# The second mixer of a two-layer diffusion backbone: its last group of modulation products behind the projections, and the output weights split on VectorE

## The chip, the core and the metric

The kernel runs on one core of one Trainium2 chip. The metric is the device time of one execution in microseconds. The program's engines are PE (TensorE, with its weight loads PEld), VectorE (DVE in the rows), ScalarE (ACT), GpSimd (POOL) and SyncE (SP), which issues nearly all DMAs from one queue in order.

## The reference

Two layers over 512 latent and 256 context tokens of width 1024. Each layer mixes (attention), adds the gated result, and passes the tokens through a mixture of 32 experts (2 per token). The second layer's mixer and its modulation are what matters here:

```python
mod = jax.nn.silu(c) @ w_mod[l] + b_mod[l]            # 1024 -> 6 * 1024, for c and for c_ctx
sh1, sc1, gt1, sh2, sc2, gt2 = jnp.split(mod[:, None, :], 6, axis=-1)
h_lat = modulate(x, norm_mix[l], sh1, sc1)
...
q, k, v = jnp.split(h @ w_in, 3, axis=-1)             # 8 heads, q and k in two halves of 64, v of 128
...
s = jnp.einsum('bqhcd,bkhcd->bhcqk', qi, k) * scale
p = jax.nn.softmax(s, axis=-1)
a = p[:, :, 0] - lam * p[:, :, 1]                     # differential attention
return jnp.einsum('bhqk,bkhe->bqhe', a, v)
...
x = x + gt1 * (rms_norm(o, subln) * (1 - lam_init)) @ w_out
tokens = modulate(x, norm_ffn[l], sh2, sc2)
x = x + gt2 * hier_moe(tokens, ...)
```

## The kernel before, in words

The stages follow one another: first mixer, its output projection with the router, experts, second mixer (`mixer_c`), its output projection, experts.

In `mixer_c` the normalised and modulated tokens are transposed and split into a high and a low part (`chh`, `chl`). For each of 8 heads, `in_proj` multiplies them by the head's weights (`wh`, `wl`; lines L264 to L266 by the helper `mm3`, three matmuls for one product at full precision) into one PSUM bank `pp`, which ScalarE empties (L689, L690). GpSimd applies the rope, VectorE the norm, and PE transposes the keys (`ptk`, L727) and, in `pack_q`, the queries (`ptq`, L582, from `qdup`). The attention runs in 32 units (8 heads by 4 tiles of 128 tokens). A unit has two score blocks on PE (L599 to L607), each followed by the maximum on VectorE (`nbias`, L1935), a scaling (L1945) and the exponential on ScalarE (L1939); then VectorE forms the factor `cf` (L1948, L1949) and the difference `p` (L1952), PE transposes it (`ptp`, L621), VectorE or ScalarE copies it (`pts`, L625), and PE multiplies it with the values (`po`, L636). VectorE normalises (L1964). Units of one head run beside the projections of later heads, so the projections end some way before the last units. When a tile of tokens has all heads, VectorE computes its norm (L287 to L299) and scales it (L1978).

Into this the mixer takes two jobs for the stage behind it. `mod_later` computes the columns of the modulation that `mixer_c` itself does not need, in groups of 2048 columns: group (1,1) holds `gt1` and `sh2`, group (1,2) `sc2` and `gt2`. A group has 8 blocks of weights of 1 MB, loaded by `mod_load` (L379) into the buffers `wr` (four, shared with the projection weights), multiplied on PE by `mod_mm` (L384, tile `pmod`), summed in pairs in a PSUM bank and added by VectorE into a row (L478). Group (1,2) is then scaled by the norm's gain (L494). SP stores the row (L500, `modrow`); the output projection reads it back (L1262 and L506). `prepare_out` loads the output weights (L1050, four blocks of 1 MB) and splits them in `split_ops`: ScalarE writes the high part (L325), another engine subtracts it from the weight (L328, tile `wo`).

The order of PE, VectorE, ScalarE and GpSimd is made at build time by the class `Sched`: each piece has an engine, an assumed duration, what it depends on, tokens that it takes and gives (`wr` for a weight buffer, `pt` and `pp` for PSUM banks, `mw` for modulation blocks in flight), and a position. An engine that is free takes the ready piece with the lowest position; unit j has position j. The modulation pieces are spread evenly from CM0 to CM1, and CMW is the number of `mw` tokens. On the chip each engine runs its list in order and waits by semaphores. The order of SP's queue is made by the framework.

Of the kernel before, what the change touches and what calls it, by code (L numbers as in the profile page):

```python
# [20 lines left out]
KD = 8  # L21
# [61 lines left out]
CPREP = 3.79  # L83
CPACK = 0.8
CP0 = -37.415
CMW = 1
CM0 = 1.0
CM1 = 28.601
DPE = .217
DDVE = 0.15  # L90
DACT = .119
# [147 lines left out]
class Backbone:  # L239
# [197 lines left out]
        return self.mod_columns(0, lambda: st["row"], [a], psp, tag)  # L437


    def mod_later(self, jobs, rows_tile, nf, silp, psp, tag, first, end, after):  # L440
        nc, S = self.nc, self.S
        total, n, out = KD * len(jobs), 0, {}
        ready = S.op("POOL", 0.5, lambda: self.mod_sil(silp), [after], pos=first)
        mms = [ready] * LA
        for l, g in jobs:
            st = {}
# [19 lines left out]
                st[k] = self.mod_load(l, g, k)  # L466

            def mm(k, st=st):
                if k % 2 == 0:
                    st["ps"] = psp.tile([128, 512], F32, tag=tag, name="pmod")  # L470
                self.mod_mm(st["ps"], silp, st[k], k, k % 2 == 0, k % 2 == 1)

            def add(k, l=l, g=g, st=st):
                r = st["row"]
                if k == 1 and (l, g) == (1, 0):
                    nc.vector.tensor_copy(r, st["ps"])
                else:
                    nc.vector.tensor_tensor(r, st["ps"], r, op=OP.add)  # L478

            S.pos = first + (end - first) * n / total  # L480
            a = S.op("POOL", 0.4, rows, [ready], take=("mrow",))
            a = S.op("DMA", 0.3, biases, [a])
            for k in range(KD):
                S.pos = first + (end - first) * n / total
                n += 1
                ld = S.op("DMA", 2.95, lambda k=k, load=load: load(k), [mms[-LA]], take=("wr", "mw"))
                mms.append(S.op("PE", 1.0, lambda k=k, mm=mm: mm(k), [ld, mms[-1]], take=() if k % 2 else ("pt",), give=("wr", "mw")))
                if k % 2:
                    a = S.op("DVE", 0.62, lambda k=k, add=add: add(k), [mms[-1], a], give=("pt",))
            if (l, g) == (1, 0):  # L490
                out[l, g] = self.mod_columns(l, lambda st=st: st["row"], [a], psp, tag, ("mrow",))
                continue
            if g == 2:
                a = S.op("DVE", 0.62, lambda st=st: nc.vector.scalar_tensor_tensor(  # L494
                    st["row"][0:64], st["row"][0:64], 1.0, nf[0:64], op0=OP.add, op1=OP.mult), [a])
# [518 lines left out]
    def prepare_out(self, l, wout, pos, after):  # L1014

        nc, S, i = self.nc, self.S, self.i
# [28 lines left out]
        for q in range(4):  # L1045
            S.pos = pos + 2 * q

            def load(q=q):
                w = parts[q] = self.wtile().rearrange("p (k f) -> p k f", k=2)
                nc.sync.dma_start(w, wout[q * 256:(q + 1) * 256].rearrange("(k p) f -> p k f", p=128))  # L1050

            ld = S.op("DMA", 2.95, load, [start], take=("wr",))
            for k in range(2):
                self.split_ops(lambda q=q, k=k: (*self.wo[2 * q + k], parts[q][:, k]), 1024, [ld], give=("wr",) if k else (),
                               low_on="POOL" if l else "DVE")


    def out_proj(self, l, oo, first, gain=None):
# [764 lines left out]
    def mixer_c(self, oo):  # L1823
        nc, tc, i = self.nc, self.tc, self.i
        S = self.S = Sched((DPE, DDVE, DACT, DPOOL), (EPE, EDVE, EACT, EPOOL), wr=NW, pt=2, s=2, po=1, pp=1, p0=2, p1=2, pts=2, qdup=1, qhl=2, rt=1, rt1=1, hss=2, khl=1,
                           grp=2, vv=3, whl=5, mrow=2, mw=CMW)
        keep, st = ExitStack(), ExitStack()
# [73 lines left out]
        for g in range(7):  # L1901
# [5 lines left out]

        room = [oo[:, 4 + m // 2, 512 * (m % 2):512 * (m % 2) + 512] for m in range(4)]
        rows = iter(room[0:2])
        self.mod_later([(1, 1), (1, 2)], lambda: next(rows), room[2], room[3][:, 0:256].rearrange("p (k f) -> p k f", k=KD),  # L1910
                       psm, "pt", CM0, CM1, S.op("-", 0.0, lambda: None, spare))
        prev = dict.fromkeys(("s", "t", "v"))
        packed, squares = {}, {t: [] for t in range(4)}
        for j, (g, t) in enumerate(units):
# [162 lines left out]
```

## Time and profile before

| | |
|---|---|
| median of 3 runs | 2040.12 us (2039.37 to 2042.49) |
| the profiled execution | 2038.13 us, its span 2036.3 us |
| PE, VectorE, ScalarE, GpSimd busy | 1767.3, 1023.2, 560.2, 355.5 us |
| granted TensorE clock, mean | 0.953 |
| second mixer, its output projection | from about 1031 us, from 1444.2 us |

The profile is one execution. Busy times are sums over the span; a stage's limit is read from its own stretch. Durations of matmuls overlap one another, so what a matmul costs is read from the starts of its neighbours. A wait is put down to what ended last.

### The profile page before, as it was taken

Reading aid. Unit: us, or ns where it says so; the run is one execution under the profiler, and the core shown is the slowest. Engines: PE = TensorE matmul, PEld = TensorE weight load, DVE = VectorE, ACT = ScalarE, POOL = GpSimd, SP = SyncE. Lnnn points to the kernel's source line nnn. Section 1 sums busy time; section 2 is a strip of 40 time slices with the busy share of each in tenths; the row PEclk is TensorE's granted clock in tenths of the full one; section 3 lists DMA queues with packets and bytes.
Section 4 is the critical chain, followed back from the end, with each engine's and each line's share of the span. In section 5 each row is a group of like instructions: output and inputs, shape, how many; then the busy total and the mean of one; then the engine's idle time right before and its main releaser. Section 6 shows DMA issues by size and latency. Waiting matters only on the chain. (4 is left out here: it accounts for less than half of the span.)

```text
span 2036.3 us, 27809 instructions
## 1 busy us (share of the span) xinstructions
PE 1767.3 (87%) x10130; PEld 1013.7 (50%) x10130; DVE 1023.2 (50%) x2621; ACT 560.2 (28%) x1280; POOL 355.5 (17%) x373
## 2 busy tenths in 40 slices
PE   4999998895999898998939999996878998988986
PEld 2798776684233222222228898885752332222222
DVE  4698878596333332323357877777782211211211
ACT  4564556321110000000054555554311100000000
POOL 2000000012122211111112222224112221111111
PEclk7999999897999999999969999998888999999999
DMA  8502314437999999999932223231459999999996
GB/s 341 198 24 94 125 46 166 155 126 272 348 387 402 408 407 409 407 406 407 360 109 74 78 102 112 73 125 42 178 203 362 383 404 413 410 413 413 410 411 254
DMA packets 98782, 532.42 MB, mean 261 GB/s; under 512 B 22840, under 2 KB 23208, under 8 KB 43344
## 3 DMA queue, kind: packets, MB, share of 16 engines
q1 hardware_dynamic: 82544, 509.53, 62.8%
q0 software_dynamic: 16096, 21.05, 4.3%
q8 instruction: 82, 1.34, 0.3%
q14 instruction: 60, 0.49, 0.1%
HBM read 517.45 MB, written 29.03 MB: 268 GB/s over the span
## 5 line engine op out<-in xcount | busy, mean ns | idle before, releaser
L1617 PE MATMUL h<-wr,x 128*64 128x512 f32 x2000 | 530.2, 612 | 91.4 <-DMA wr<-in_w_dram 89.3
L1617 PEld LDWEIGHTS h<-wr,x 128*64 128x64 f32 x2000 | 147.9, 138 | 403.8 <-issue 227.8
L1603 DVE COPY x<-trx 128x512 f32<-128x512 f32 (+1 forms) x67 | 43.7, 659 | 458.8 <-PE trx L1598 452.6
L1617 PE MATMUL py<-wr,gt 128*64 128x512 f32 x1024 | 240.4, 599 | 2.4 <-DMA wr<-in_w_dram 1.7
L1672 ACT ACTIVATE sl<-h 64x512 f32<-64x512 f32 x64 | 37.8, 591 | 701.6 <-PE h L1617 701.5
L264 PE MATMUL pp<-wh,chh 128*128 128x384 f32 (+1 forms) x384 | 133.0, 346 | 5.5 <-ACT vv L690 3.7
L1617 PEld LDWEIGHTS py<-wr,gt 128*64 128x64 f32 x1024 | 68.5, 136 | 137.6 <-issue 121.3
L1677 DVE TENSOR_TENSOR gp<-sl,h 64x512 f32<-64x512 f32 x64 | 67.9, 1061 | 122.5 <-ACT sl L1672 121.8
L266 PE MATMUL pp<-wh,chl 128*128 128x384 f32 (+1 forms) x384 | 123.9, 323 | 0.9 <-DVE chl L328 0.9
L265 PE MATMUL pp<-wl,chh 128*128 128x384 f32 (+1 forms) x384 | 123.7, 322 | 0.0
L621 PE MATMUL ptp<-cst,p 128*128 128x128 f32 x592 | 97.7, 286 | 24.0 <-DVE p L1952 11.5
L1520 POOL DMA_INDIRECT xg<-h2d,ridx x64 | 68.1, 1065 | 276.4 <-PE trx L1598 236.8
L1532 DVE SCALAR_TENSOR_TENSOR y<-py,rsw,g 128x512 f32<-128x512 f32 x64 | 48.0, 751 | 126.5 <-PE py L1617 126.5
L1526 POOL DMA_INDIRECT xd<-y,ridx x32 | 53.5, 1671 | 234.5 <-DVE y L1536 146.7
L621 PEld LDWEIGHTS ptp<-cst,p 128*128 128x128 f32 x592 | 70.7, 145 | 43.6 <-issue 17.6
L1526 POOL DMA_INDIRECT out_dram<-y,ridx x32 | 52.0, 1624 | 215.9 <-DVE y L1532 168.5
L264 PEld LDWEIGHTS pp<-wh,chh 128*128 128x128 f32 x384 | 74.0, 193 | 16.9 <-ACT vv L690 7.9
L1191 POOL TENSOR_TENSOR h2p<-xi,bc 128x512 f32<-128x512 f32 x10 | 16.0, 1601 | 375.5 <-DVE xi L1188 350.0
L944 ACT ACTIVATE p<-s,nbias,r 128x256 f32<-128x256 f32 (+3 forms) x96 | 76.5, 799 | 18.0 <-DVE nbias L938 8.0
L625 ACT COPY pts<-ptp 128x384 f32<-128x384 f32 (+2 forms) x116 | 55.9, 487 | 76.1 <-PE ptp L621 75.4
L926 DVE TENSOR_REDUCE nbias<-s 128x1 f32<-128x768 f32 (+3 forms) x80 | 64.7, 814 | 18.9 <-PE s L607 16.7
L265 PEld LDWEIGHTS pp<-wl,chh 128*128 128x128 f32 x384 | 74.1, 193 | 0.0
(348 smaller groups left out, 3293.8 us busy)
## 6 DMA issues: line engine op xcount, KB each, us to landing
wr<-in_w_dram SPq DMA_DIRECT2D x378, 1024.0 KB
wr<-in_w_mod_dram SPq DMA_DIRECT2D x48, 1024.0 KB
wr<-in_wc_dram SPq DMA_DIRECT2D x16, 768.0 KB
wr<-in_wab_dram SPq DMA_DIRECT2D x8, 768.0 KB
oo<-in_w_dram SPq DMA_DIRECT2D x6, 1024.0 KB
h2d<-h2p SPq DMA_DIRECT2D x10, 512.0 KB
bc<-modrow SPq DMA_DIRECT2D x9, 512.0 KB
wr<-in_w_out_ab_dram SPq DMA_DIRECT2D x4, 1024.0 KB
```

The source lines that it names most:

```text
L264: mm(ps, xh, wh, start=start, stop=False)
L265: mm(ps, xh, wl, start=False, stop=False)
L266: mm(ps, xl, wh, start=False, stop=stop)
L621: nc.tensor.transpose(st[g][:, b], st["p"][:, (g + b) * 128:(g + b + 1) * 128], self.id)
L625: f(st["pts"][:, g:g + n], st[g][:, :n])
L926: nc.vector.tensor_reduce(nb(), st["s"][:, off:off + w].rearrange("p (n f) -> p n f", n=n), axis=AX.X, op=OP.max, negate=True)
L944: nc.scalar.activation(p[:, a:b], st["s"][:, a:b], AF.Exp, bias=nb()[:, m:m + 1], scale=hr()[:, m:m + 1], accum_out=z["ssum"][:, h + m:h + ...
L1520: nc.gpsimd.indirect_dma_start(out=dst, out_offset=None, in_=rows(self.h2d[l], n), in_offset=bass.IndirectOffsetOnAxis(ap=idx, axis=0), bo ...
L1526: nc.gpsimd.indirect_dma_start(out=rows(sums, n), out_offset=bass.IndirectOffsetOnAxis(ap=idx, axis=0), in_=src, in_offset=None, bounds_ch ...
L1532: nc.vector.scalar_tensor_tensor(dst, src, sw[:, 0], g[0], op0=OP.mult, op1=OP.mult)
L1617: mm(out[0][CS * m:CS * m + CS], at(k), w(m, k), start=k == 0, stop=k == n - 1, tile_position=(0, CS * m), skip_group_check=True)
L1677: nc.vector.tensor_tensor(x["p"][dst].rearrange("t (k p) -> t p k", k=4), v(a), v(b), op=OP.mult)
```

## The change

`mod_later` is called twice. Group (1,1) has positions from 1.0 to 24.0 and sums pairs of blocks in a bank `pt` as before. Group (1,2) has positions from 26.8 to 29.0, begins when group (1,1) is stored, and sums all of its 8 blocks (`run=KD`) in the projections' bank `pp`, so that VectorE adds once. Two blocks may be in flight instead of one (CMW). In `prepare_out` the low part of the output weights is computed by VectorE in the second layer too. The first mixer's calls give the same pieces as before. Lines of the changed kernel are 2 or 3 higher than before.

```diff
--- before.py
+++ after.py
@@ -83,9 +83,11 @@
 CPREP = 3.79
 CPACK = 0.8
 CP0 = -37.415
-CMW = 1
+CMW = 2
 CM0 = 1.0
-CM1 = 28.601
+CM1 = 24.0
+CM2 = 26.8
+CM3 = 29.0
 DPE = .217
 DDVE = 0.15
 DACT = .119
@@ -437,10 +439,10 @@
         return self.mod_columns(0, lambda: st["row"], [a], psp, tag)
 
 
-    def mod_later(self, jobs, rows_tile, nf, silp, psp, tag, first, end, after):
+    def mod_later(self, jobs, rows_tile, nf, silp, psp, tag, first, end, after, run=2, go=()):
         nc, S = self.nc, self.S
         total, n, out = KD * len(jobs), 0, {}
-        ready = S.op("POOL", 0.5, lambda: self.mod_sil(silp), [after], pos=first)
+        ready = S.op("POOL", 0.5, lambda: self.mod_sil(silp), [after], pos=first) if not go else S.op("-", 0.0, lambda: None, go, pos=first)
         mms = [ready] * LA
         for l, g in jobs:
             st = {}
@@ -466,13 +468,13 @@
                 st[k] = self.mod_load(l, g, k)
 
             def mm(k, st=st):
-                if k % 2 == 0:
+                if k % run == 0:
                     st["ps"] = psp.tile([128, 512], F32, tag=tag, name="pmod")
-                self.mod_mm(st["ps"], silp, st[k], k, k % 2 == 0, k % 2 == 1)
+                self.mod_mm(st["ps"], silp, st[k], k, k % run == 0, k % run == run - 1)
 
             def add(k, l=l, g=g, st=st):
                 r = st["row"]
-                if k == 1 and (l, g) == (1, 0):
+                if k < run and (l, g) == (1, 0):
                     nc.vector.tensor_copy(r, st["ps"])
                 else:
                     nc.vector.tensor_tensor(r, st["ps"], r, op=OP.add)
@@ -484,9 +486,9 @@
                 S.pos = first + (end - first) * n / total
                 n += 1
                 ld = S.op("DMA", 2.95, lambda k=k, load=load: load(k), [mms[-LA]], take=("wr", "mw"))
-                mms.append(S.op("PE", 1.0, lambda k=k, mm=mm: mm(k), [ld, mms[-1]], take=() if k % 2 else ("pt",), give=("wr", "mw")))
-                if k % 2:
-                    a = S.op("DVE", 0.62, lambda k=k, add=add: add(k), [mms[-1], a], give=("pt",))
+                mms.append(S.op("PE", 1.0, lambda k=k, mm=mm: mm(k), [ld, mms[-1]], take=() if k % run else (tag,), give=("wr", "mw")))
+                if k % run == run - 1:
+                    a = S.op("DVE", 0.62, lambda k=k, add=add: add(k), [mms[-1], a], give=(tag,))
             if (l, g) == (1, 0):
                 out[l, g] = self.mod_columns(l, lambda st=st: st["row"], [a], psp, tag, ("mrow",))
                 continue
@@ -1052,7 +1054,7 @@
             ld = S.op("DMA", 2.95, load, [start], take=("wr",))
             for k in range(2):
                 self.split_ops(lambda q=q, k=k: (*self.wo[2 * q + k], parts[q][:, k]), 1024, [ld], give=("wr",) if k else (),
-                               low_on="POOL" if l else "DVE")
+                               low_on="DVE")
 
 
     def out_proj(self, l, oo, first, gain=None):
@@ -1907,8 +1909,9 @@
 
         room = [oo[:, 4 + m // 2, 512 * (m % 2):512 * (m % 2) + 512] for m in range(4)]
         rows = iter(room[0:2])
-        self.mod_later([(1, 1), (1, 2)], lambda: next(rows), room[2], room[3][:, 0:256].rearrange("p (k f) -> p k f", k=KD),
-                       psm, "pt", CM0, CM1, S.op("-", 0.0, lambda: None, spare))
+        silp = room[3][:, 0:256].rearrange("p (k f) -> p k f", k=KD)
+        made = self.mod_later([(1, 1)], lambda: next(rows), room[2], silp, psm, "pt", CM0, CM1, S.op("-", 0.0, lambda: None, spare))
+        self.mod_later([(1, 2)], lambda: next(rows), room[2], silp, psp, "pp", CM2, CM3, None, KD, [made[1, 1]])
         prev = dict.fromkeys(("s", "t", "v"))
         packed, squares = {}, {t: [] for t in range(4)}
         for j, (g, t) in enumerate(units):
```

The order of PE where the projections end, before. `pp` are the projections, `s` scores, `ptq` and `ptk` transposed queries and keys, `ptp` the transposed difference of a unit, `po` its product with the values:

```order
L265 MATMUL pp<-wl,chh 128x384
L266 MATMUL pp<-wh,chl 128x384
L599 MATMUL s<-kt,qh 128x512
L604 MATMUL s<-kt,ql 128x512
L606 MATMUL s<-kt,qh 128x256
L607 MATMUL s<-kt,ql 128x256
L582 MATMUL ptq<-cst,qdup 128x128 x4
L621 MATMUL ptp<-cst,p 128x128 x6
L582 MATMUL ptq<-cst,qdup 128x128 x2
L636 MATMUL po<-vv,pts 128x128 x6
L727 MATMUL ptk<-cst,khl 128x128 x4
L599 MATMUL s<-kt,qh 128x512
```

The same place in the changed kernel. A row `pmod` with x4 here is one of the eight products (8 matmul rows in the trace):

```order
L268 MATMUL pp<-wh,chl 128x384
L601 MATMUL s<-kt,qh 128x512
L606 MATMUL s<-kt,ql 128x512
L608 MATMUL s<-kt,qh 128x256
L609 MATMUL s<-kt,ql 128x256
L584 MATMUL ptq<-cst,qdup 128x128 x2
L386 MATMUL pmod<-wr,oo 32x512 x8
L584 MATMUL ptq<-cst,qdup 128x128 x2
L623 MATMUL ptp<-cst,p 128x128 x6
L584 MATMUL ptq<-cst,qdup 128x128 x2
L638 MATMUL po<-vv,pts 128x128 x6
L386 MATMUL pmod<-wr,oo 32x512 x4
```

Two products (`x8`) stand behind the first scores and one between `po` and `ptk`, which is the next row; five more follow before the mixer's end. Before, all sixteen stood among the `pp` rows; now eight do.

The order of VectorE behind the last unit's difference `p`, before. `rs...` and `oss` are the norm of a tile, `oo<-oo,oss` its scaling, `ol` the low part of the output projection's input:

```order
L1978 TENSOR_TENSOR oo<-oo,oss 128x1024
L296 TENSOR_TENSOR rsq<-rsy 128x8
L288 TENSOR_SCALAR rsy<-rsv 128x8
L297 TENSOR_TENSOR rsq<-rsq,rsv 128x8
L289 TENSOR_SCALAR rsy<-rsy 128x8
L299 SCALAR_TENSOR_TENSOR oss<-rsq,rsy 128x8
L296 TENSOR_TENSOR rsq<-rsy 128x8
L1964 TENSOR_SCALAR oo<-po,rz 128x128
L1978 TENSOR_TENSOR oo<-oo,oss 128x1024
L297 TENSOR_TENSOR rsq<-rsq,rsv 128x8
L287 TENSOR_SCALAR rsv<-oss 128x8
L1122 SCALAR_TENSOR_TENSOR ol<-ot,sub,oh 128x512
```

The same place in the changed kernel, up to the first `ol`:

```order
L330 TENSOR_TENSOR wo<-wr,wo 128x1024
L299 TENSOR_TENSOR rsq<-rsq,rsv 128x8
L298 TENSOR_TENSOR rsq<-rsy 128x8
L330 TENSOR_TENSOR wo<-wr,wo 128x1024
L1967 TENSOR_SCALAR oo<-po,rz 128x128
L301 SCALAR_TENSOR_TENSOR rsy<-rsq,rsy 128x8
L299 TENSOR_TENSOR rsq<-rsq,rsv 128x8
L330 TENSOR_TENSOR wo<-wr,wo 128x1024
L298 TENSOR_TENSOR rsq<-rsy 128x8
L301 SCALAR_TENSOR_TENSOR rsy<-rsq,rsy 128x8
L289 TENSOR_SCALAR rsv<-oss 128x8
L1124 SCALAR_TENSOR_TENSOR ol<-ot,sub,oh 128x512
```

Three subtractions `wo` stand here, ahead of `ol`, and the second scaling has gone behind it. The other five stand ahead of the last unit's difference. GpSimd's list has none any more.

The order of SP's queue before, with the last projection weights, the end of the modulation, the output weights (`in_w_out_c`), the early expert weights (`in_w_dram`) and the reads of the stored rows:

```order
L1756 DMA wr<-in_wc_dram 128x1536 x2
L379 DMA wr<-in_w_mod_dram 128x2048 x3
L1050 DMA wr<-in_w_out_c_dram 128x2x1024 x4
L500 DMA modrow_88<-oo 2x512 x4
L1033 DMA rwrt<-in_w_group_dram 128x8x4
L1034 DMA rwrt<-in_w_expert_dram 128x8x32
L1035 DMA rbrt<-in_b_group_dram 128x4
L1036 DMA rbrt<-in_b_expert_dram 128x32
L1247 DMA wr<-in_w_dram 128x2048 x4
L1262 DMA mrows<-modrow_88 8x128 x2
L506 DMA bc_13261<-modrow_88 128x1024
```

The same in the changed kernel:

```order
L1758 DMA wr<-in_wc_dram 128x1536 x6
L381 DMA wr<-in_w_mod_dram 128x2048 x4
L1035 DMA rwrt<-in_w_group_dram 128x8x4
L1036 DMA rwrt<-in_w_expert_dram 128x8x32
L1037 DMA rbrt<-in_b_group_dram 128x4
L1038 DMA rbrt<-in_b_expert_dram 128x32
L1052 DMA wr<-in_w_out_c_dram 128x2x1024
L381 DMA wr<-in_w_mod_dram 128x2048 x2
L1052 DMA wr<-in_w_out_c_dram 128x2x1024 x3
L1249 DMA wr<-in_w_dram 128x2048
L502 DMA modrow_88<-oo 2x512 x4
L1249 DMA wr<-in_w_dram 128x2048 x2
```

The blocks of group (1,2) now stand behind all projection weights, two of them behind the first output weight, and the store of the row behind all four output weights and one expert load.

## Rows read from the trace of the kernel before

**Rows 1.** This view is the page, part 1: engine, busy us (share of the span) and number of instructions.

```profile
PE 1767.3 (87%) x10130; PEld 1013.7 (50%) x10130; DVE 1023.2 (50%) x2621; ACT 560.2 (28%) x1280; POOL 355.5 (17%) x373
```

**Rows 2.** This view is busy time by stretch (from:to in us, length; then PE, PEld, VectorE, ScalarE and GpSimd busy us with the number of instructions, the granted TensorE clock, the DMA share and GB/s): the projections of the second mixer, and the stretch from their end to the output projection.

```profile
1082.00:1391.50 309.50, 300.56 (x2039) 271.31 (x2039) 240.11 (x682) 162.54 (x403) 79.84 (x127) 1.00 0.27 93
1391.50:1444.20 52.70, 31.28 (x148) 26.00 (x146) 40.54 (x107) 24.21 (x51) 23.43 (x16) 0.71 0.26 84
```

**Rows 3.** This view is waits of PE from 1391.5 to 1444.2 us: the waiting line, what it waited for, us in total, times, longest us.

```profile
PE ptp L621 <- DVE p L1952: 11.3, 3, 5.0
PE ptq L582 <- DVE qdup L577: 4.4, 2, 2.4
```

**Rows 4.** This view is the tile `pmod` (sums of the modulation in PSUM) from 1082 to 1392 us: engine, operation, count: min/median/max ns, first and last start us, shapes.

```profile
L384 PE MATMUL pmod<-wr,oo x128: 592/605/617, 1082.8 to 1368.6; 128*32 128x512 f32 x128
L478 DVE TENSOR_TENSOR oo<-pmod,oo x8: 677/681/692, 1095.3 to 1369.3; 128x512 f32<-128x512 f32 x8
```

**Rows 5.** This view is the timeline of PE at the first of these products: start us, length us, engine, line, operation, out<-in, shapes, count (eight matmul rows merged).

```profile
1082.34 0.34 PE L265 MATMUL pp<-wl,chh 128*128 128x384 f32 x1
1082.52 0.33 PE L266 MATMUL pp<-wh,chl 128*128 128x384 f32 x1
1082.78 1.07 PE L384 MATMUL pmod<-wr,oo 128*32 128x512 f32 x8
1083.78 0.45 PE L264 MATMUL pp<-wh,chh 128*128 128x384 f32 x1
1084.07 0.34 PE L265 MATMUL pp<-wl,chh 128*128 128x384 f32 x1
```

**Rows 6.** This view is the timeline of SP's queue: start us, us from the first to the last issue of the merged entry, line, out<-in, count.

```profile
1092.54 2.68 SPq L1756 DMA_DIRECT2D wr<-in_wc_dram  x2
...
1133.57 1.47 SPq L1756 DMA_DIRECT2D wr<-in_wc_dram  x2
...
1347.47 22.18 SPq L1050 DMA_DIRECT2D wr<-in_w_out_c_dram  x4
...
1414.52 21.86 SPq L1247 DMA_DIRECT2D wr<-in_w_dram  x4
1443.47 0.64 SPq L1262 DMA_DIRECT2D mrows<-modrow  x2
```

**Rows 7.** This view is busy time by stretch, as in rows 2, in slices of 1 us behind the issue at 1414.52 us of a load of 1 MB.

```profile
1418.50:1419.50 1.00, 1.00 (x7) 0.86 (x6) 0.98 (x5) 0.03 (x1) 1.00 (x2) 0.77 0.18 74
1419.50:1420.50 1.00, 1.00 (x11) 1.00 (x10) 1.00 (x2) 1.00 (x3) 1.00 (x1) 1.00 0.00 0
```

**Rows 8.** This view is the tile `wo` (split output weights) over the whole span, so of both mixers; columns as in rows 4.

```profile
L328 DVE TENSOR_TENSOR wo<-wr,wo x8: 1211/1214/1215, 320.3 to 340.9; 128x1024 fp32r<-128x1024 f32 x8
L328 POOL TENSOR_TENSOR wo<-wr,wo x8: 2337/2364/2369, 1409.8 to 1433.7; 128x1024 fp32r<-128x1024 f32 x8
```

**Rows 9.** This view is groups of VectorE from 1409 to 1437 us, shapes kept apart: line, operation, out<-in, count | busy us, mean ns | idle time before them.

```profile
L1952 DVE SCALAR_TENSOR_TENSOR p<-p,cf 128x768 f32<-128x768 f32 x4 | 5.9, 1472 | 0.0
L1935 DVE TENSOR_REDUCE nbias<-s 128x1 f32<-128x768 f32 x6 | 5.7, 955 | 3.2 <-PE s L607 3.2
L1945 DVE TENSOR_TENSOR nbias<-nbias,r 128x1 f32<-128x1 f32 x6 | 3.1, 527 | 0.0
...
L1949 DVE SCALAR_TENSOR_TENSOR cf<-rz,lam,ssum 128x1 f32<-128x1 f32 x4 | 2.6, 656 | 0.0
L288 DVE TENSOR_SCALAR rsy<-rsv 128x8 int32<-128x8 int32 x2 | 2.5, 1240 | 0.0
L289 DVE TENSOR_SCALAR rsy<-rsy 128x8 int32<-128x8 int32 x2 | 1.2, 598 | 0.0
```

**Rows 10.** This view is the timeline of VectorE behind it; columns as in rows 5.

```profile
1425.00 0.14 DVE L1945 TENSOR_TENSOR nbias<-nbias,r 128x1 f32<-128x1 f32 x1
...
1436.66 0.21 DVE L1949 SCALAR_TENSOR_TENSOR cf<-rz,lam,ssum 128x1 f32<-128x1 f32 x1
...
1436.95 1.01 DVE L1952 SCALAR_TENSOR_TENSOR p<-p,cf 128x768 f32<-128x768 f32 x1
...
1440.92 0.17 DVE L288 TENSOR_SCALAR rsy<-rsv 128x8 int32<-128x8 int32 x1
...
1442.86 1.21 DVE L1978 TENSOR_TENSOR oo<-oo,oss 128x1024 f32<-128x1024 f32 x1
...
1444.19 0.75 DVE L1122 SCALAR_TENSOR_TENSOR ol<-ot,sub,oh 128x512 fp32r<-128x512 f32 x1
```

**Rows 11.** This view is line L494 over the whole span; columns as in rows 4.

```profile
L494 DVE SCALAR_TENSOR_TENSOR oo<-oo x1: 682/682/682, 1370.0 to 1370.0; 64x512 f32<-64x512 f32 x1
```

**Rows 12.** This view is busy time by stretch, as in rows 2, at the end of the mixer.

```profile
1437.00:1444.20 7.20, 5.52 (x26) 4.91 (x26) 5.66 (x23) 2.01 (x7) 0.00 (x0) 0.59 0.43 148
```

**Rows 13.** This view is the timeline of PE behind the end of the projections; columns as in rows 5, the idle time before it and its cause in brackets.

```profile
1395.08 0.66 PE L582 MATMUL ptq<-cst,qdup 128*128 128x128 f32 x2 [2.40 <-DVE qdup L577]
1398.25 1.51 PE L621 MATMUL ptp<-cst,p 128*128 128x128 f32 x6 [2.52 <-DVE rsq L296]
...
1400.17 2.32 PE L636 MATMUL po<-vv,pts 128*128 128x128 f32 x12
1402.34 0.60 PE L727 MATMUL ptk<-cst,khl 128*128 128x128 f32 x4
1403.85 0.50 PE L599 MATMUL s<-kt,qh 128*128 128x512 f32 x1 [0.91 <-ACT kt L732]
```


## The prediction

> **What bounds the kernel now.** I read the page's busy times first [rows 1]: PE is busy for 87% of the span, VectorE for half of it. That average hides stages, so the next view is the table of busy times by stretch [rows 2]. The second mixer has two parts. From 1082 to 1391.5 us PE is busy for 300.56 of 309.5 us at full clock: PE sets the time, and its idle time is 2.9%. Then the projections are over, and until 1444.2 us, when the output projection begins, PE is busy for 31.28 of 52.7 us at a granted clock of 0.71, while VectorE is busy for 40.54. I call this second part the tail. The waits of PE in it [rows 3] say what sets it: the longest are for `p` L1952 and `qdup` L577, both VectorE's. So PE's work is worth its whole price before 1391.5 and little in the tail; VectorE's is hidden before and on the path in the tail. The change moves PE work from the first part into the second and swaps what disturbs VectorE there.
>
> **The eight products of group (1,2) leave the projections.** Before, sixteen products of the modulation stand among the projections, 8 matmul rows each, 128 in all [rows 4]. What one costs is read from starts, since matmuls overlap [rows 5]: the projection matmul ahead starts at 1082.52, the first one behind at 1083.78, the next at 1084.07. Undisturbed, this run of matmuls steps by 0.18 us (1082.34, 1082.52). So 1.26 − 0.18 = 1.08 us for the product and 0.29 − 0.18 = 0.11 us for the first matmul behind it, 1.2 us together. Eight make 9.6 us. As 2.9% of this stretch is idle anyway, I give back that share, 0.3 us: **−9.3 us**. The bounds are −9.6 and 0; zero would be if another engine set this stretch, but VectorE is at 240.11 of 309.5 us [rows 2] and loses work too: of eight additions of 0.68 us [rows 4] the last group's four go from here and come back as one in the tail.
>
> **Group (1,1) and the loads before the tail.** With two loads in flight instead of one, group (1,1) is done earlier, and its loads stand ahead of later projection weights on SP's queue. In the order two of those weights now wait for a third and a fourth product, some 50 PE rows after the second. In the trace that pair was issued from 1092.54 us and the next pair 41 us later, from 1133.57 [rows 6], so a pair has most of a head's time to land. A load of 1 MB takes 4 us from issue to landing: issued at 1414.52, it still moved data in the slice to 1419.5 and none after [rows 6, 7]. A shift of some 10 us is covered; I cost it at nothing. Without cover it would cost 4 us once.
>
> **VectorE in the tail: what leaves.** GpSimd's eight subtractions of 2.36 us [rows 8] go. While they ran, small VectorE instructions took far too long: between 1409 and 1437 us L1945 had a mean of 527 ns, L1949 656, L288 1240, L289 598 and L1952 1472 [rows 9]; with GpSimd idle the same take 0.14, 0.21, 0.17, 0.17 and 1.01 us (L289, like L288, is a one-scalar operation of the same shape) [rows 10]. The excess is 6 × 0.387 + 4 × 0.446 + 2 × 1.07 + 2 × 0.43 + 4 × 0.46 = 9.0 us. L1935, a reduction from PSUM, stays at 955 ns and was not disturbed. The rule on this is in the Trainium skill, "SBUF — State Buffer", Who interferes with whom: a VectorE instruction with two SBUF inputs and a GpSimd instruction that reads SBUF exclude one another for the whole instruction, and a reduction is never touched. The reduction agrees. Taken at its fullest the rule would let all 8 × 2.36 = 18.9 us of GpSimd block VectorE, and the sum below would be lower by another 9.9 us; the rows show 9.0, so I take 9.0.
>
> **VectorE in the tail: what comes.** The same subtraction takes VectorE 1.21 us, as the first mixer's rows show [rows 8]. Five of the eight stand ahead of the last unit's L1952 in the new order: 6.1 us. With them come one addition of the modulation (0.68 us [rows 4]) and its scaling L494 (0.68 us [rows 11]). Up to the last L1952 that is −9.0 + 6.1 + 1.4 = −1.5 us. Behind it, before, 6.2 us passed from its end (1436.95 + 1.01) to the first `ol` L1122 at 1444.19 [rows 10]; three subtractions (+3.6) now stand there and one of two L1978 (−1.2) moves behind `ol`. VectorE had 1.5 us free there (7.2 us less 5.66 us busy, from the window 1437 to 1444.2 [rows 12]), so I count +0.9. Together **−0.6 us**. Bounds: −9.0, if all the stalls were on the path and the new work falls into VectorE's idle 12.2 us of the tail (52.7 − 40.54 [rows 2]); +11.1 (8 × 1.21 + 1.4), if the stalls were not on it and the work is. The rows of the waits lie nearer the first end, but the new work is as long as the stalls, hence a value near zero.
>
> **PE in the tail.** Eight products of 1.08 us are 8.6 us against 21.4 us of PE's idle time. The first two stand behind the first scores, where PE waited 2.40 and 2.52 us [rows 13]. The third now stands between `po` L636 and `ptk` L727, which before followed at once (1400.17 + 2.32 against 1402.34): it holds up the keys of the last heads, **+1.1 us**. The fourth stands where PE waited 0.91 us for those keys; the other four stand where it waited 11.3 us for `p` [rows 3]. Bounds 0 and +8.6.
>
> **Loads in the tail.** Four of the last group's blocks can be in the four `wr` buffers before the projections end. The other four, and the four output weights that before were issued from 1347.47 us on [rows 6], take turns in those buffers, each behind the product or subtraction that frees one. On SP, behind the waits for those buffers, stand the store of the modulation rows, three of the six early expert loads and the reads of the stored rows; those reads were issued only at 1443.47 us [rows 6], late in the tail anyway. Blocks five and six are issued within some 4 us of the projections' end and used after the first scores at +12.3 us (1403.85 − 1391.5 [rows 13]). I cost the loads at nothing; without cover each is 4 us [rows 6, 7].
>
> **The sum.** −9.3 − 0.6 + 1.1 = −8.8 us. The profiled execution took 2038.13 us (span 2036.3), so 2029.3; the median of the runs, 2040.12, is 2.0 above it: **2031.3 us**. The experts behind are shifted whole: their stream of weights starts when the output projection frees its buffers.
>
> **Rivals.**
> *Given back in the tail (0.16).* VectorE takes all eight subtractions on the path without the stalls having cost what I think, or the products hold the scores: the tail grows by about 9 us, and the time is 2040. For it: VectorE is the busiest engine of the tail already. Against: the 9.0 us of excess sit in `cf`, `p` and `nbias`, for which PE and ACT wait.
> *The weights come late: slower (0.08).* PE takes its matmuls in order. If a product's block is not there, all scores behind it wait. The last two blocks stand on SP behind the first output weight, which waits for the third product; from there block seven, block eight and two output weights come one after another, 4 × 4.0 us = 16 us of landings. If they show in full, the time is 2031.3 + 16 = 2047. It decides when PE reaches the seventh product earlier than about 8 us after the fourth; by the tail's pace of a unit in some 10 us (40 us from 1403.85 to 1444 for four) it should not. The Trainium skill, "TensorE: Matmul & The Clock Gate", What happens when you issue a matmul, says that only weight loads are pulled ahead and matmuls stay in program order; that speaks against putting a product with a late operand here.
> *The tail's clock recovers (0.08).* The granted clock is 1.00 where PE is busy 97%, and 0.71 in the tail [rows 2], a mix of 1.2 and 2.4 GHz. Filled with 8.6 us more work it may stay at 2.4 GHz: 31.28 us of work would take 31.28 × 0.71 = 22.2 us, 9.1 us less. With half of it on the path the time is 4.5 us lower, 2026.8. The Trainium skill, "TensorE: Matmul & The Clock Gate", What's actually happening, states that the slow clock is the idle state and activity releases it.
>
> **Chances.** My forecast has 0.68. The range 2023.0 to 2039.0 takes in the clock's case with some of the stalls' bound below, and above a tail that grows by 8 us; it leaves out the late weights and about half of "given back". A run of this kernel can tell 0.2%, some 4 us, from no change. Faster by more: forecast and clock, 0.76; within: 0.16; slower: 0.08.
>
> **What would show it.** In the new profile: `pmod` products ending before some 1200 us and again from the projections' end on; the projections ending near 1382 us; no GpSimd subtraction and L288, L1945, L1949 at 0.14 to 0.22 us in the tail; eight `wo` rows of 1.21 us on VectorE; a tail of 51 to 54 us. I am wrong if PE waits for `in_w_mod_dram` there, if the projections end later than 1386, or if the tail passes 58 us.

## The result and the profile after

The changed kernel took 2026.44 us (median of 4 runs, 2025.14 to 2028.59) against 2039.74 us (4 runs) for the kernel before: 13.3 us less, ratio 0.9931 with a 95% interval of 0.9918 to 0.9943. The forecast was 2031.3. The profiled execution took 2027.06 us (span 2025.2). It lies above its median and that of before below its own, so the two profiles are only 11.1 us apart.

All times by stage below are differences of starts on PE's timeline: projections, from the first `pp` to the first score behind the last; tail, from there to the first `pop` (`pop` are the sums of the output projection in PSUM); output projection, from there to its last `pop`.

| us | before | changed |
|---|---|---|
| projections | 346.61 (from 1044.98) | 336.55 (from 1044.36) |
| tail | 52.67 | 49.01 |
| output projection | 59.18 (from 1444.26) | 60.83 (from 1429.92) |

So 10.1 us come from the projections and 3.7 from the tail, and the output projection gives 1.65 back. The first part of the projections, up to the first product of the modulation, is the same in both kernels (140 rows of PE) and took 37.8 us before and 39.1 us here, at a granted clock of 0.79 and 0.72; from the first product on it is 308.8 us before and 297.4 us here, 11.4 less. The output projection's first 10 us ran at a granted clock of 1.00 before and of 0.83, a mix of 1.2 and 2.4 GHz, here (the clock is the third number from the end):

```profile
1444.26:1454.30 10.04, 10.01 (x58) 7.38 (x59) 8.79 (x31) 1.75 (x3) 0.00 (x0) 1.00 0.91 339
1429.92:1440.00 10.08, 9.88 (x51) 7.00 (x52) 8.62 (x34) 1.75 (x3) 0.00 (x0) 0.83 0.93 323
```

The busy time of the changed kernel by stretch, which answers to [rows 2]:

```profile
1082.00:1380.90 298.90, 292.18 (x1979) 270.47 (x1978) 240.00 (x683) 159.63 (x398) 79.63 (x129) 1.00 0.21 68
1380.90:1429.90 49.00, 35.72 (x211) 24.11 (x211) 38.14 (x109) 26.13 (x54) 4.76 (x8) 0.83 0.68 240
```

PE has 4.4 us more to do in the tail, VectorE 2.4 less, and the granted clock is 0.83 instead of 0.71. The groups of VectorE in the tail, which answer to [rows 9] (L1955 was L1952, L1948 was L1945, L290 was L288):

```profile
L330 DVE TENSOR_TENSOR wo<-wr,wo 128x1024 fp32r<-128x1024 f32 x8 | 9.7, 1216 | 0.0
L1938 DVE TENSOR_REDUCE nbias<-s 128x1 f32<-128x768 f32 x9 | 8.4, 952 | 7.8 <-PE s L609 7.8
L1955 DVE SCALAR_TENSOR_TENSOR p<-p,cf 128x768 f32<-128x768 f32 x5 | 5.5, 1099 | 0.0
...
L1948 DVE TENSOR_TENSOR nbias<-nbias,r 128x1 f32<-128x1 f32 x9 | 1.4, 152 | 0.0
...
L290 DVE TENSOR_SCALAR rsy<-rsv 128x8 int32<-128x8 int32 x4 | 0.9, 228 | 0.0
```

The eight subtractions are here at 1.216 us, and every small row is near what it took beside an idle GpSimd [rows 10]. The waits of PE there, which answer to [rows 3]:

```profile
PE ptp L623 <- DVE rsy L301: 3.7, 1, 3.7
PE ptp L623 <- DVE rsq L298: 2.8, 1, 2.8
PE s L601 <- ACT p L1942: 2.4, 3, 1.4
PE pop L266 <- DVE wo L330: 1.7, 1, 1.7
PE ptp L623 <- DVE p L1955: 1.7, 1, 1.7
```

Of the 11.3 us for `p` 1.7 are left. The same row `ptp` waits another 6.5 us, put down to the norm, where it was 2.52 before [rows 13]. None of these waits is for `in_w_mod_dram`. PE's timeline at the third product:

```profile
1389.52 2.77 PE L638 MATMUL po<-vv,pts 128*128 128x128 f32 x12
1392.22 1.75 PE L386 MATMUL pmod<-wr,oo 128*32 128x512 f32 x8
1393.90 0.66 PE L729 MATMUL ptk<-cst,khl 128*128 128x128 f32 x4
1394.49 1.06 PE L386 MATMUL pmod<-wr,oo 128*32 128x512 f32 x8
```

It stands where it was forecast, between `po` and `ptk`. It took 1.75 us and the next product 1.06: from 1387.6 us on, behind a wait of 2.83 us, the granted clock was 0.50 (1.2 GHz), in the stretch of the third product (1392.22 to 1393.90) it was 0.58, and then 1.00 (2.4 GHz).

### The profile page after: what moved, and what is told of

Same layout as the page of the kernel before. It is cut to its first block, busy times and chain, and to the rows that moved or that the text cites. A ratio compares the mean times of both kernels' runs of the same rounds, so it can differ in the third digit from the quotient of the medians.

```text
span 2025.2 us, 27795 instructions
## 1 busy us (share of the span) xinstructions
PE 1767.7 (87%) x10130; PEld 1013.8 (50%) x10130; DVE 1022.0 (50%) x2628; ACT 559.3 (28%) x1278; POOL 335.7 (17%) x365
## 5 line engine op out<-in xcount | busy, mean ns | idle before, releaser
L1674 ACT ACTIVATE sl<-h 64x512 f32<-64x512 f32 x64 | 37.8, 591 | 702.7 <-PE h L1619 696.0
L1534 DVE SCALAR_TENSOR_TENSOR y<-py,rsw,g 128x512 f32<-128x512 f32 x64 | 48.1, 751 | 126.4 <-PE py L1619 124.7
L1528 POOL DMA_INDIRECT out_dram<-y,ridx x32 | 52.7, 1646 | 216.0 <-DVE y L1534 177.3
L266 PEld LDWEIGHTS pp<-wh,chh 128*128 128x128 f32 x384 | 74.7, 195 | 11.4 <-ACT vv L692 7.4
L268 PEld LDWEIGHTS pp<-wh,chl 128*128 128x128 f32 x384 | 74.3, 193 | 1.4 <-DVE chl L330 1.4
```

The costliest lines, as they stand in the source:

```text
L266: mm(ps, xh, wh, start=start, stop=False)
L268: mm(ps, xl, wh, start=False, stop=stop)
L1528: nc.gpsimd.indirect_dma_start(out=rows(sums, n), out_offset=bass.IndirectOffsetOnAxis(ap=idx, axis=0), in_=src, in_offset=None, bounds_ch ...
L1534: nc.vector.scalar_tensor_tensor(dst, src, sw[:, 0], g[0], op0=OP.mult, op1=OP.mult)
```

## The experiments

My theory: the projections give up PE's time of the eight products, and the tail gives up stalls of VectorE beside GpSimd. A rival: the products keep PE's clock up in the tail. The measured values together (time: median and number of runs; intervals are of the ratio to the kernel before on the same chip). E3, E4 and E8 leave group (1,2)'s products out, which changes what the experts get; only their stages are compared. The stages are read from one profiled execution each. "From first product" is the part of the projections from the first product of the modulation on. Ahead of it stand the same 96 `pp` in every kernel, and they took 36.6 to 39.1 us from execution to execution, so up to 2.5 us of a difference in the column "projections" can come from there and not from the experiment. Behind it, executions of one order agree within 0.1 us (before, E2 and E5; changed, E1, E4 and E11).

| | time, us | ratio, 95% | projections | from first product | tail |
|---|---|---|---|---|---|
| before | 2039.74 (4) | | 346.6 | 308.8 | 52.7 |
| changed | 2026.44 (4) | 0.9918 to 0.9943 | 336.6 | 297.4 | 49.0 |
| E1 move alone | 2036.16 (10) | 0.9970 to 0.9989 | 335.1 | 297.4 | 57.8 |
| E2 split alone | 2034.92 (10) | 0.9964 to 0.9983 | 346.9 | 308.9 | 48.2 |
| E3 before, no products (1,2) | | | 344.7 | 305.8 | 53.1 |
| E4 changed, no products (1,2) | | | 335.3 | 297.5 | 48.3 |
| E5 GpSimd writes only | 2027.16 (1) | | 347.4 | 308.9 | 40.2 |
| E6 pairs in `pt` | 2029.07 (4) | 0.9922 to 0.9955 | 342.3 | 303.6 | 48.1 |
| E7 short banks, before* | 2036.60 (10) | 0.9969 to 0.9989 | 344.7 | 306.9 | 51.4 |
| E8 as E3, no banks | | | 342.6 | 304.9 | 52.9 |
| E9 short banks, changed | 2025.19 (4) | 0.9908 to 0.9941 | 334.7 | 295.8 | 48.1 |
| E10 one in flight | 2045.50 (8) | 1.0017 to 1.0039 | 336.4 | 298.4 | 46.8 |
| E11 four subtractions late | 2029.80 (4) | 0.9934 to 0.9967 | 334.0 | 297.4 | 47.3 |
| E12 the same behind `ol` | 2022.75 (5) | 0.9902 to 0.9929 | 334.6 | 295.8 | 47.6 |

*In E7 no score follows the last `pp` at once; its projections are taken to the row behind (`ptp`) and hold four rows of scores (some 0.7 us) more than those of the others, its tail as many fewer.

**E1 and E2: each half alone.**

```diff
 E1: all of the change, but
+                               low_on="POOL" if l else "DVE")
 E2: before, but
-                               low_on="POOL" if l else "DVE")
+                               low_on="DVE")
```

> The change without its second part: the last group's products stand behind the projections, GpSimd still splits the output weights. Two theories for the tail (from the end of the projections to the first output projection matmul: 52.7 us before, 49.0 us changed). Theory A: GpSimd's subtractions hold VectorE on the path, and taking them away shortens the tail. Then here the projections end about 10 us earlier as in the change, the stalls stay (L290 and L1948 well over 0.5 us in the mean) and the tail is 53 to 56 us; time 2030 to 2033. Theory B: the products fill PE's idle time and raise its granted clock, and that shortens the tail. Then the tail is 48 to 50 us with the stalls in it, and the time is about that of the change, 2026 to 2028.

> The kernel before with the second part of the change alone: VectorE splits the second mixer's output weights, all sixteen products stay among the projections. Theory A (stalls on the path): the projections end as before (near 1391.5 us), the tail falls from 52.7 to 45 to 48 us, and the time to 2033 to 2036. Theory B (the products raise the clock): the tail stays at 51 to 54 us, the time at 2038 to 2041. My recorded sum for this part alone is -0.6 us.

The halves are worth 4.4 and 5.6 us (medians against 2040.53 beside them), together 10.0; the change is worth 13.3. By the tails alone, 52.7 + 5.1 (E1) − 4.4 (E2) would be 53.4, and it is 49.0. E1 has the whole gain of the projections and gives 5.1 us of it back in the tail, more than theory A allowed (53 to 56 us); E2's tail is just outside its 45 to 48. VectorE's groups in the tail of E1:

```profile
L299 DVE TENSOR_TENSOR rsq<-rsq,rsv 128x8 f32<-128x8 f32 x12 | 6.5, 553 | 0.1
L298 DVE TENSOR_TENSOR rsq<-rsy 128x8 f32<-128x8 f32 x13 | 6.2, 490 | 0.1
L1981 DVE TENSOR_TENSOR oo<-oo,oss 128x1024 f32<-128x1024 f32 x3 | 5.8, 1922 | 0.0
L1955 DVE SCALAR_TENSOR_TENSOR p<-p,cf 128x768 f32<-128x768 f32 x5 | 5.5, 1099 | 0.0
L290 DVE TENSOR_SCALAR rsy<-rsv 128x8 int32<-128x8 int32 x5 | 3.2, 630 | 0.1
```

Two blocks of the group stand ahead of the later output weights on SP, and GpSimd's subtractions run until 54 us into the tail (44 before). They now meet the norm (L290 to L301, L1981) instead of `p`, which is back at 1.1 us. Behind the norm stands the first `pop`, and PE waited there:

```profile
PE pop L266 <- DVE rsq L298: 10.7, 1, 10.7
PE ot L1110 <- DVE rsy L290: 6.5, 1, 6.5
```

**E3 and E4: the same orders without the eight products.**

```diff
-            def mm(k, st=st):
+            def mm(k, l=l, g=g, st=st):
+                if (l, g) == (1, 2):
+                    return
```

The additions of that group are left out in the same way.

> The kernel before, with the products and additions of the group (1,2) left out, its loads and everything else in the same order (so the expert stage gets other rows and is not compared). Price of the eight products among the projections: the recorded estimate is 9.6 us at most, 9.3 with PE's idle share. If the products cost just PE's time, the projections end 9 to 10 us earlier than before (near 1382) and the tail stays at 52 to 54 us. If the bank that each pair holds also delays transposes, they end 10.5 to 13 us earlier.

> The changed kernel, with the products and the addition of the group (1,2) left out, its loads and everything else in the same order (so the expert stage is not compared). Price of the eight products in the tail. Theory A: they only delay the keys of the last heads, by about 2 us; the tail falls from 49.0 to 46 to 48 us. Theory B (they keep the clock up): the granted clock of the tail falls from 0.83 to 0.7 to 0.75, and the tail is 49 to 53 us without them.

E4 ends the rival of the clock as the cause of the shorter tail: with no product in it the clock was 0.72, as theory B expected, but the tail took 48.3 us, no longer than with them. Between E4 and the change the products cost 0.7 us (48.27 to 49.01); E9, which has them in its tail too and nearly the same order, took 48.1 at a clock of 0.89, so no price of theirs is told apart from what the clock does from one execution to another. They bring 8.6 us of work at full clock, but PE's busy time in the tail rose by only 5.0 us (30.7 to 35.7) as the clock went from 0.72 to 0.83. E3 was the surprise: eight products fewer, but only 3.0 us less in the projections, counted from the first product on. PE's busy time there in the kernel before, in E3 and in the changed kernel:

```profile
1082.80:1391.60 308.80, 299.86 (x2036) 270.86 (x2036) 240.11 (x682) 162.62 (x403) 79.84 (x127) 1.00 0.27 93
```

```profile
1082.90:1388.60 305.70, 291.79 (x1971) 269.40 (x1971) 238.34 (x678) 162.50 (x403) 80.03 (x127) 1.00 0.27 94
```

```profile
1083.50:1380.90 297.40, 290.68 (x1971) 269.22 (x1971) 240.00 (x683) 159.58 (x397) 79.63 (x129) 1.00 0.21 68
```

In E3 PE had 8.1 us less to do and 5.0 us more idle time (13.9 instead of 8.9). In the changed kernel it has 9.2 us less to do and is idle for only 6.7 us. So a product that goes leaves a hole, idle time of PE, as long as the order is the one made for it.

**E6, E7, E8: is it the banks?** A pair of products holds one of two `pt` banks from its first product to the end of VectorE's addition, 10 to 27 us in the kernel before, and the transposes use the same two.

```diff
 E6: changed, but group (1,2) as
+        self.mod_later([(1, 2)], ..., silp, psm, "pt", CM2, CM3, None, 2, [made[1, 1]])
 E7: before, with the parameter run of the change and run=1 for both groups
 E8: E3, and in the order's input
+  take=() if k % 2 or (l, g) == (1, 2) else ("pt",), ...
+  give=() if (l, g) == (1, 2) else ("pt",)
```

> The change, but the eight products behind the projections go as four pairs through the two banks that transposes use, with an addition each, and not in one bank of their own. If the one bank is what makes products cheap in the tail: every pair holds one of two banks from its first product to VectorE's addition, transposes wait, and four additions of 0.7 us instead of one come to VectorE: tail 51 to 54 us beside 49.0, time 2028 to 2031. If the bank is of no account there: tail 49 to 50, time within 1 us of the change.

> The kernel before with all 16 products left where they are, but each product closes its own bank and is added at once (16 additions instead of 8), so that a bank is held for one product and one addition and not across two products some 17 us apart. Theory that the banks, not the products' own 1.2 us, cost the projections their time: heads 4 to 7 fall from 43 to about 41 us each, projections 338 to 342 us instead of 346.6, time 2032 to 2036. Rival, the products' own time on TensorE: projections 346 to 348, time 2040 to 2042 (eight more additions of 0.7 us on VectorE, which has room).

> As the kernel before without the eight products of the group (1,2) and their additions, but now the order is made as if they took no bank either (TensorE's 1.0 us for each is still reckoned in). With the banks still reckoned in, the projections took 344.7 us instead of 346.6. If the reckoned bank is what keeps the order slow: 336 to 339 us. If it is the reckoned price on TensorE, or where the order is made anew: 343 to 346 us.

The banks have a share, no more: held briefly (E7) they give 1.9 us (some 2.6 with the scores that E7 has moved ahead), where 5 to 9 were expected; not reckoned in (E8), 0.9 beyond E3 from the first product on, where 6 to 9 were expected. E6 did not do what its name says. With a `pt` bank to be had, its products went back among the projections (rows `pmod` until 1351.7 us). It is the wait for a bank `pp`, free only when the projections are over, that puts the group behind them. So E6 is an order with all sixteen products in the projections, two blocks in flight and another spread, and needs 303.6 us from the first product on: 5.2 of the 11.4 us come with another order alone, and 6.2 (303.6 to 297.4) go with the products. Its tail of 48.1 us, like E4's of 48.3, holds no product; its time came out in the expected range for another reason.

**E5: what GpSimd does to VectorE.**

```diff
 before, in low():
+            if low_on == "POOL":
+                for _ in range(2):
+                    self.nc.gpsimd.memset(st[1].bitcast(F32), 0.0)
+                return
```

> The kernel before, in which GpSimd, instead of subtracting, fills each low half of the output weights with zeros by two memsets (so the low half of the output weights is left out); everything is ordered as before. If VectorE's stalls come from GpSimd reading two inputs beside it, VectorE's small rows of the tail fall to what they took without GpSimd (L1952 1.1 us, L1945 0.15, L288 below 0.3) and the tail, 52.7 us before, ends near 47 to 48.5 (the split alone, with VectorE subtracting, had 48.2). Rival: any work of GpSimd beside it holds VectorE; then those rows stay at 0.5 to 1.5 us and the tail at 51 to 53.

GpSimd and VectorE in the tail of E5:

```profile
L330 POOL MEMSET wo<- 128x1024 f32 x16 | 15.0, 963 | 0.5
```

```profile
L1956 DVE SCALAR_TENSOR_TENSOR p<-p,cf 128x768 f32<-128x768 f32 x5 | 5.5, 1101 | 0.0
...
L1949 DVE TENSOR_TENSOR nbias<-nbias,r 128x1 f32<-128x1 f32 x9 | 1.3, 150 | 0.0
...
L288 DVE TENSOR_SCALAR rsy<-rsv 128x8 int32<-128x8 int32 x5 | 1.1, 217 | 0.0
```

The memsets read nothing and ran earlier than the subtractions do in the kernel before (1409.85 to 1436.03): from 1398.61 to 1414.08 us. Only part of the rows above stand beside them:

```profile
1398.61 15.47 POOL L330 MEMSET wo<- 128x1024 f32 x16
```

```profile
1402.04 0.60 DVE L714 COPY r<-hrr 128x4 f32<-128x4 f32 x1
...
1408.87 0.52 DVE L581 COPY qdup<-qk 128x256 f32<-128x256 f32 x1
...
1413.32 1.01 DVE L1956 SCALAR_TENSOR_TENSOR p<-p,cf 128x768 f32<-128x768 f32 x1
```

Beside the memsets one whole `p` took 1.01 us, four rows of L1949 0.15 each and one `cf` 0.21, as alone; no row of L288 stood there. But copies from SBUF to SBUF were held: `r` took 0.60 us, the second `qdup` 0.52 and `rpay` (L1446) 0.41, where the kernel before has 0.17, 0.29 and 0.17 for them with GpSimd idle. Two rows with two inputs right behind a held copy ended with it (L715 0.53 instead of 0.42, L299 0.33 instead of 0.16).

```profile
1400.67 0.17 DVE L710 COPY r<-hrr 128x4 f32<-128x4 f32 x1
```

```profile
1407.06 0.29 DVE L577 COPY qdup<-qk 128x256 f32<-128x256 f32 x1
```

So for VectorE's rows with two inputs it is GpSimd's reading that holds them, as far as these few rows show it, and writing holds copies. The tail fell by 12.5 us, further than I had expected: taking the subtractions off GpSimd is worth 12.5 us (one execution), and VectorE's own eight subtractions (E2) cost 8.0 of it again.

**E10: one block in flight.**

```diff
-CMW = 2
+CMW = 1
```

> The change, but with one block of the modulation in flight instead of two (CMW 1, as before). In the kernel with the last group left in pairs and two in flight the projections took 342.3 us, 4.3 less than before with all sixteen products still among them; in the change 336.6. Theory that the 10 us of the change are two parts, about 4 from two in flight (the members of a pair of group (1,1) stand closer, so its bank is held for less) and about 6 from the eight products that leave: projections 340 to 342 us here, time 2030 to 2032. Rival, that the products alone make it: projections 336 to 338, time within 1.5 us of the change. The tail stays at 48 to 50 us in both.

Both theories missed the main thing. The projections are nearly as short as with two in flight (1.0 us longer from the first product on), so that rival was right on them; but the kernel became slower than before, by 5.2 us. PE's waits behind the tail, and SP's queue:

```profile
PE pc L1269 <- DMA mrows<-modrow: 19.7, 1, 19.7
```

```profile
1409.96 12.79 SPq L381 DMA_DIRECT2D wr<-in_w_mod_dram  x4
1426.07 1.19 SPq L1249 DMA_DIRECT2D wr<-in_w_dram  x2
...
1429.65 5.62 SPq L1249 DMA_DIRECT2D wr<-in_w_dram  x4
1435.48 3.98 SPq L502 DMA_DIRECT2D modrow<-oo  x4
1449.30 0.26 SPq L1264 DMA_DIRECT2D mrows<-modrow  x1
```

The blocks come one after another, and the last product starts at 1428.44 us. VectorE adds it behind its rows of the norm and completes the row at 1435.74 (L496); the store, issued from 1435.48, stands behind six expert loads on SP's queue, and the row is read at 1449.30. `pc` L1269, which transposes the row read back, stands in PE's list among the `pop` rows, and these stop for 19.7 us. In the changed kernel the row is stored at 1413.64 and read at 1429.17.

**E9, E11, E12: what is left.**

```diff
 E9: changed, with run=1 for group (1,1)
 E11: changed; the subtractions of output weights 5 to 8 wait for the last unit's po;
      first tile of the output projection:
+                    order = [(m, q) for q in range(4) for m in range(2)]
 E12: E9 and E11, but these four subtractions stand behind the first tile's second ol:
+                    lows.append(S.op("DVE", 1.15, low, [halves[1]] + lows[-1:], pos=-7.0))
```

> The change, but the products of group (1,1) each close their bank and are added at once (eight additions instead of four). In the order before, the same for both groups took 1.9 us from the projections. If pairs still hold transposes up in the change: projections 334 to 336 us instead of 336.6, time 2024.5 to 2026. If two in flight have taken that away already: 336 to 338, time within 1 us of the change.

> The change, but the last four of the eight subtractions on VectorE stand behind the last unit's output, and the first tile of the output projection takes its weights in such an order that these four are needed last. Without any subtraction on VectorE (and none on GpSimd) the tail took 40.2 us, with eight on VectorE 48.2 to 49. If they lie on the path one for one: tail 44 to 46 us, some 2 us given back at the start of the output projection, where VectorE computes the first low parts; time 2023 to 2025. Rival, that four subtractions fit into VectorE's idle 10 us of the tail anyway: tail 48 to 49, time 2026 to 2029.

> The change with the short banks of group (1,1), and with the last four of the eight subtractions behind the low parts of the first output tile on VectorE (not between them, as in the last experiment), the first tile's weights again in the order that needs these four last. If what was won in the tail there (1.7 us) was lost because those subtractions held the first low parts up by 2.4 us: tail 44.5 to 46.5 us, the output projection no longer than 61.5 us from its first matmul to its last, time 2020 to 2023.5. Rival, that work taken from VectorE's tail comes back as late in the output projection, whose VectorE is busy 8.5 of 10 us: that stretch 62 to 64 us, time 2024 to 2027.

E9's projections are 1.6 us shorter from the first product on, near E7's 1.9; its time is within 1.3 us of the change and not told apart from it. E11's tail is 1.7 us shorter, not 3 to 5, and what it won was lost behind: its output projection took 62.7 us, and PE waited for `ol` (L1131), which stood behind the late subtractions:

```profile
PE ot L1117 <- DVE rsq L298: 3.0, 1, 3.0
...
PE pop L266 <- DVE rsv L289: 1.7, 1, 1.7
...
PE pop L268 <- DVE ol L1131: 1.0, 1, 1.0
```

The wait of 1.7 us at the first `pop` is as long in the change, E11 and E12, whatever row of VectorE it is put down to, so the subtraction named in the change did not make it.

E12 puts the four behind `ol`. Its output projection took 60.6 us as hoped, but the tail stays at 47.6 where 44.5 to 46.5 was expected. The last `p` starts 41.1 us into it, and in the change 40.6: as far as the rows tell, the norm has taken the place of the subtractions ahead of it, and PE waits 3.0 us for its `rsq` (L298) at `ot`, the transposes of the normalised tokens. 2022.75 us is the lowest median of all and in the expected range; its interval overlaps that of the change, so the 3.7 us between them are likely and not shown.

## Why the prediction was right, and where not

*What bounds the stages.* "PE sets the time" in the projections was half of it. PE is busy 97% there, yet E3 took 8.1 us of its work away and got 3.0. The order that was made around the products, and the waits that it fixes, hold the rest.

*Eight products leave, −9.3.* Measured −11.4 from the first product on (−10.1 by the whole stage), the projections ending at 1380.9 where "near 1382" stood. PE's busy time fell by 9.2 us (8.1 in E3), so the price of the products was about right; its idle time fell by 2.2, where I had given 0.3 back. The reason was incomplete: the price comes back only with an order made without these products, and in the old order the same step is worth 3.0 (E3), so that the sum came near is partly luck. E6 splits it: about 5 us for another order with all products still in, about 6 for their leaving. What exactly in the old order costs those 5 us stays open; short banks are worth about 2 (1.9 in E7, 1.6 in E9), two blocks in flight instead of one 1.0 (E10).

*Group (1,1) and the loads before the tail, 0.* No wait of PE for them. Its last product starts at 1196 us, where in the old order it was at 1227.

*VectorE in the tail, −0.6.* This is the step that was mis-sized. Without modulation's 1.4 us it said −2.0; E2 measured −4.4. "Leaves" was 9.0 and is 12.5 (E5); "comes" was 7.0 and is 8.0 (E2 less E5). I had added up how much longer VectorE's rows were. From before to E5 VectorE's busy time fell by 8.7 us (40.54 to 31.86), close to my 9.0, but the tail by 12.5. PE's busy time fell as well, 31.28 to 25.71, at a granted clock of 0.83 instead of 0.71; that the rest comes of three engines waiting for one another in turn is likely and not shown. The bound of −9.0 for the whole term held. On the fullest reading of the rule in the Trainium skill, "SBUF — State Buffer", Who interferes with whom, the sum would have been 9.9 us lower; the runs bear out 3.5 us of these 9.9 (12.5 instead of 9.0). The same section says that a GpSimd instruction that only writes does not contend with such a VectorE instruction; E5 agrees (0.15 us for L1949 and 1.01 for `p` beside the memsets).

*PE in the tail, +1.1, and the addition and scaling.* Expected +2.5 together, measured +0.7 (E4 to the change), which the clock's changes cover. In E1 the same move lengthens the tail by 5.1 us (52.7 to 57.8), as it puts GpSimd's subtractions off into the norm: it is cheap only since GpSimd is out of the way. So the two parts of the change are not independent, and the sum of terms could not show that.

*The tail.* "51 to 54 us" was wrong: 49.0, by the terms above. Against the sum the tail gave 4.2 us more (−3.7 instead of +0.5) and the projections 0.8 more; the output projection took 1.65 back.

*Behind the tail.* The sum had no term for the output projection. It took 1.65 us more, at a granted clock of 0.83 in its first 10 us; E9, with the same wait of 1.7 us ahead of it, had 1.00 there and took 59.4 us.

*Loads in the tail, 0.* Right, with two in flight. Without that the kernel takes 19 us more (E10, 2045.5 against 2026.4).

*The rivals.* "Given back" is what E1 does, not the change. "The weights come late" had its price about right (16 us) and its mechanism partly: the blocks do come one after another, but with one in flight, and what waits is not a score but the row's way through DRAM; I had called those reads "late in the tail anyway". "The clock recovers" gave 2026.8, nearly the measured time, for another reason: the clock did rise, to 0.83, but E4 has the short tail at 0.72 and E1 the longest at 0.86. As far as busy times tell, the higher clock takes in part of the products' own work (5.0 us more of busy time for 8.6 of work).

## What to carry to other kernels

When work leaves a stage whose order is made at build time, price it against an order made without it: rows taken out of the old order left 5.0 of their 8.1 us as holes. Compare stages from a mark behind which executions of one order agree: here the part ahead of it varied by 2.5 us. A stall that one engine puts on another can cost more than the excess of the stalled rows (12.5 against 9.0 us here), and moving other work can shift it onto a later, barer part of the path, so two such edits are to be tried together as well as apart. For work moved late, follow its result to its last reader: here a row completed late and stored behind other loads on one queue cost 19 us, more than all else.

## What the runs showed of the hardware that was not expected

GpSimd's writes, 16 memsets of 128x1024 with a mean of 963 ns, left VectorE's rows with two inputs as they are alone (0.15 and 1.01 us), but held its copies from SBUF to SBUF (`qdup` 0.52 us instead of 0.29, `r` 0.60 instead of 0.17). Its subtractions made even a one-scalar operation on 128x8 (L290 in E1) take 630 ns in the mean instead of 228. GpSimd pays too: its subtractions in E1 took 2.37 us in the median and 3.32 once:

```profile
L330 POOL TENSOR_TENSOR wo<-wr,wo x8: 2342/2372/3317, 1405.7 to 1431.3; 128x1024 fp32r<-128x1024 f32 x8
```
